# Splitting a matmul's first loads over two queues, and loading the last weight columns as float32

## Chip, cores and metric

The kernel runs on one core of a Trainium2 chip. The metric is the device time of one execution in microseconds (us), inputs and output in the chip's main memory. Before the change the median of three runs is 360.94 us (360.82 to 362.36).

## What is computed

x is 16 x 512 x 768 and w_qkv 768 x 2304, both float32. The product is cut into three column ranges, stacked as the output:

```python
qkv = np.matmul(x, w_qkv)
q, k, v = qkv[..., :768], qkv[..., 768:1536], qkv[..., 1536:]
return np.stack([q, k, v], axis=0).astype(np.float32)
```

## The kernel before

x is seen as 8192 rows of 768: 64 row tiles of 128, taken in 32 pairs p with r = 0 or 1. The contraction of 768 is cut into six slices j of 128. w's 2304 columns are five parts: four column blocks of 512 (q = 0 or 1 for a quad of two, c = 0 or 1 for the block within it) and a remainder of 256 columns in the middle, w_rem, held in two tiles of three slices each as bf16.

From pair 2 on, a pair and a quad are multiplied by a scheme of seven half-size products (`do`, lines 255 to 282, `product`, line 233) on sums of parts of x (`sums_x`) and of w (`sum_w`, line 112); products 1 and 2 use bf16, the others float32 data. The remainder columns are done plainly by `rem` and `rem_row` (lines 297 to 316): six bf16 matmuls of 256 columns for each row tile. Pairs 0 and 1 are multiplied plainly in bf16 by `block` (line 438), one column block at a time and slice by slice, as w's slices arrive.

The order of all instructions is written by hand: the program order of each engine is the order of the calls, and semaphores are put in where data depends. SyncE (SP) does little else than issue DMAs, so its program order is the order of its queue; ScalarE (ACT) and GpSimd (POOL) have queues of their own, and what they issue stands in line with their computing instructions. Hardware DMAs, whoever issues them, take eight completion semaphores in turn, so an issue also waits for the transfer eight before it.

What happens at the start, which the change and the prediction speak of:

- Line 397: DVE clears a tile of zeros, with which PE does matmuls for warming up (`busy`, line 423), eight at first and one or two between later steps.
- Lines 398 to 406: SP loads the four row tiles of pairs 0 and 1 (`load_row`, line 159). ScalarE issues two small loads, "touch", one of a few columns of w and one of a few columns of x's third row tile; nothing reads them.
- Lines 407 to 409: SP loads w's column block 0 in seven pieces, the first slice halved, and block 1 in six (`load_slices`).
- Line 410: SP loads the two row tiles of pair 2 in eight parts (`load_x_rows`, line 131), in another arrangement that DVE turns in blocks (`transpose`, line 148, instruction line 154).
- Lines 412 to 421: `hold` makes POOL wait for a transfer by copying one column of it (line 414). POOL waits for the first slice of w's block 1, then issues two loads of w_rem (line 419), which cast float32 to bf16 on the way. It waits for the first tile of pair 2 and goes on. SP loads quad 1's block 0 (`load_blocks`).
- Lines 495 to 514: for each of the four row tiles, DVE and ScalarE cast a half each to bf16 (`cast_row`, instruction lines 166 and 167), PE transposes six pieces (`turn_row`, line 184), and DVE and ScalarE copy the halves out of the PSUM banks (166, 167). DVE casts w's slices (line 434).
- Line 515: the first `block`, PE's line 456. Then four evacuations on ScalarE (line 446), two casts of w's slices by ScalarE (line 432), the second block (line 526), and `rem` for pairs 0 and 1 (line 529, PE's line 299).
- Lines 530 to 539: pair 2 is turned in two parts, ScalarE evacuates the second block's tiles, rounds each part of pair 2 to bf16 (`round_row`, line 200) and copies the remainder's results out (line 313).
- Lines 555 to 562: PE does the seven products of pair 2 and quad 0: 1 and 2 (evacuated at line 253), the remainder of pair 2, then product 6, which is added into the bank that line 253 has read (line 268).

From pair 3 on, `two` repeats one order for each pair, and `last` does the last.

Of the kernel before, what the change touches and what calls it, by code (L numbers as in the profile page):

```python
# [10 lines left out]
def kernel(  # L11
# [20 lines left out]
    nc = tc.nc  # L32
    P = 128
    G = 32
# [4 lines left out]
    KT = K // P  # L39
    KH = KT // 2  # L40
# [3 lines left out]
    REM = N3 - 4 * CB  # L44
    Q_OFF = (0, 2 * CB + REM)
    R_OFF = 2 * CB
    fp32 = mybir.dt.float32
    f32r = mybir.dt.float32r
    bf16 = mybir.dt.bfloat16
    ident = mybir.ActivationFunctionType.Identity  # L50
# [3 lines left out]
    x_flat = x.rearrange("b t h -> (b t) h")  # L54
# [7 lines left out]
    o_pool = ctx.enter_context(tc.tile_pool(name="o", bufs=5))  # L62
# [7 lines left out]
    m_pool = ctx.enter_context(tc.tile_pool(name="m", bufs=2))  # L70
# [6 lines left out]
    w_rem = [w_pool.tile([P, KH, REM], bf16, name="w_rem0"), None]  # L77
# [13 lines left out]
    def load_w(dst, j0, nj, off, cols):  # L91
        rows = w_qkv.rearrange("(p j) n -> p j n", j=KT)
        nc.sync.dma_start(dst, rows[:, j0:j0 + nj, off:off + cols])

    stage = {}

    def load_slices(c, cuts):
        t = tq_pool.tile([P, KT, CB], fp32, name="st0", tag="tq")
        stage[0, 0, c], stage[0, 1, c] = t[:, :KH, :], t[:, KH:, :]
        for j, nj, lo, hi in cuts:  # L100
            load_w(t[:, j:j + nj, lo:hi], j, nj, Q_OFF[0] + c * CB + lo, hi - lo)
# [10 lines left out]
    def sum_w(q, n):  # L112
        t1, t2, t3, t4 = ts[q]
        o, in0, in1 = {
            1: (t1, stage[q, 0, 1], stage[q, 0, 0]),
            2: (t2, stage[q, 1, 1], t1),
            3: (t3, stage[q, 1, 1], stage[q, 0, 1]),
            4: (t4, stage[q, 1, 0], t2),
        }[n]
        nc.vector.tensor_tensor(o, in0, in1, op=sub)  # L120

    xin, xf, xb, sr = {}, {}, {}, {}
# [8 lines left out]
    def load_x_rows(p, parts=range(8)):  # L131
        if p not in xin:
            xin[p] = xin_pool.tile([P, 2 * P // G, KC], fp32, name="xin")
        rows = x_flat[p * 2 * P:(p + 1) * 2 * P, :].rearrange("(g b) k -> b g k", b=G)
        for n in parts:
            r, i = divmod(n, 4)
            gs = slice(r * P // G, (r + 1) * P // G)
            nc.sync.dma_start(
                xin[p][i * G:(i + 1) * G, gs], rows[:, gs, i * KC:(i + 1) * KC]
            )  # L140
# [15 lines left out]

    def load_row(p, r):
        if r == 0:  # L160
            xin[p] = xin_pool.tile([P, 2, K], fp32, name="xin")
        row = (2 * p + r) * P
        nc.sync.dma_start(xin[p][:, r], x_flat[row:row + P, :])  # L163

    def copy_halves(dst, src):
        nc.vector.tensor_copy(out=dst[0], in_=src[0])
# [26 lines left out]
    act, dve = nc.scalar, nc.vector  # L193
# [202 lines left out]
    zero = xb_pool.tile([P, CB], bf16, name="zero", tag="xb")  # L396
    nc.vector.memset(zero[:], 0.0)
    load_row(0, 0)
    touch = m_pool.tile([P, 2, G], fp32, name="touch")
    nc.scalar.dma_start(touch[:, 0], w_qkv.rearrange("(p j) n -> p j n", j=KT)[:, 0, :G])  # L400
    nc.scalar.dma_start(touch[:, 1], x_flat[2 * P:3 * P, :G])
    nc.scalar.activation(tiny[:], zero[:, :1], ident)
    make_identity(nc, eye)
    load_row(0, 1)
    load_row(1, 0)
    load_row(1, 1)
    half = CB // 2
    load_slices(0, [(0, 1, 0, half), (0, 1, half, CB)] + [(j, 1, 0, CB) for j in range(1, KT)])
    load_slices(1, [(j, 1, 0, CB) for j in range(KT)])
    load_x_rows(2)  # L410

    def hold(src):
        mark = m_pool.tile([P, 1], fp32, name="mark")
        nc.gpsimd.tensor_copy(out=mark[:], in_=src)  # L414

    hold(stage[0, 0, 1][:, 0, :1])
    for h in range(2):
        rows = w_qkv.rearrange("(p j) n -> p j n", j=KT)[:, h * KH:(h + 1) * KH]
        nc.gpsimd.dma_start(w_rem[h][:], rows[:, :, R_OFF:R_OFF + REM])  # L419
    hold(xin[2][:, 0, :1])  # L420
    load_blocks(1, 0)

# [6 lines left out]
    def cast_j(q, c, w, j, eng=act, n=slice(0, CB)):  # L429
        src = stage[q, j // KH, c][:, j % KH, n]  # L430
        if eng is act:
            eng.activation(w[:, j, n], src, ident)
        else:
            eng.tensor_copy(out=w[:, j, n], in_=src)
# [86 lines left out]
    cast_j(0, 1, bt, 3, dve)  # L521
    cast_j(0, 1, bt, 4, act)
    cast_j(0, 1, bt, 5, act)
    sum_w(0, 2)
    nc.gpsimd.tensor_copy(out=b22[0][:], in_=stage[0, 1, 1])
    late = block(
# [119 lines left out]
```

## Time and profile before

| what | us |
|---|---|
| median of three runs | 360.94 (360.82 to 362.36) |
| the profiled execution | 360.69 |
| its span, first to last instruction | 358.9 |
| PE busy | 352.3 (98%) |
| DVE, ACT, POOL busy | 227.4, 185.7, 178.6 |
| first matmul of the first block (line 456) | 8.45 |
| first matmul of the remainder (line 299) | 18.85 |

The span is what the profile covers; 1.8 us of the execution lie around it. The page gives busy time of each engine, then the chain of work that ended last, then groups of instructions. The timeline lists instructions of one line together: start, duration, engine, line, operation, tiles written and read, shape, count, and in brackets the idle time of the engine before them and what ended it. A DMA is listed where it is issued; the list of issues, taken over a window that holds one, tells how long that one took to land. A view by stretches gives each engine's busy time, the granted clock, the share of the DMA engines in use and GB/s.

### The profile page before, as it was taken

How to read it: one execution, taken by the hardware profiler on the slowest of the kernel's cores; microseconds unless marked ns; L12 is line 12 of the kernel's file. 1: busy time of each engine (PE TensorE's matmuls, PEld its weight loads, DVE VectorE, ACT ScalarE, POOL GpSimd, SP SyncE). 2: the span in 40 equal slices, each digit the busy share in tenths (PEclk: the TensorE clock that was granted, in tenths of full speed). 3: DMA queues.
4: the chain of work that ended last, by engine and by line, in shares of the span. 5: the costliest groups of instructions: out<-in, count | busy, mean ns of one | idle time of the engine just before them, and what ended most of it. 6: DMA issues, size and time to landing. Idle time of an engine off the chain costs nothing.

```text
span 358.9 us, 5279 instructions
## 1 busy us (share of the span) xinstructions
PE 352.3 (98%) x1780; PEld 251.0 (70%) x1780; DVE 227.4 (63%) x244; ACT 185.7 (52%) x316; POOL 178.6 (50%) x187
## 2 busy tenths in 40 slices
PE   7999999999999999999999999999999999999995
PEld 3465577777777777777777777777777777777764
DVE  3879676676556675556676556676556676556643
ACT  5469644445444445444445544445545445545443
POOL 0221866435665444665444665444665444666420
PEclk9999999999999999999999999999999999999999
DMA  7999999798999999899999999988999899989767
GB/s 276 345 368 347 329 360 369 242 347 285 288 300 312 294 289 274 295 293 316 294 293 274 293 290 319 295 274 293 295 283 322 294 298 271 296 278 325 290 239 258
DMA packets 82106, 107.73 MB, mean 300 GB/s; under 512 B 5408, under 2 KB 62240, under 8 KB 82080
## 3 DMA queue, kind: packets, MB, share of 16 engines
q1 hardware_dynamic: 66672, 96.35, 82.4%
q10 hardware_dynamic: 14608, 10.65, 9.1%
q0 software_dynamic: 800, 0.39, 0.8%
q8 instruction: 14, 0.23, 0.3%
q14 instruction: 12, 0.10, 0.1%
HBM read 32.28 MB, written 75.50 MB: 300 GB/s over the span
## 4 chain that ended last, share of the span: by engine, by line
PE 92%; DMA 5%; ACT 1%; ACTq 0%; POOL 0%; SPq 0%; issue 0%
PE ps L244 78%; PE ps L299 11%; PE ps L456 3%; DMA w_rem<-in_w_qkv_dram 2%; DMA xin<-in_x_dram 1%; DMA st<-in_w_qkv_dram 1%; SPq L163 0%; ACT o L279 0%; ACTq L354 0%; POOL w_rem L419 0%; ACT orem L368 0%; POOL mark L414 0%; ACTq L370 0%; ACTq L368 0%
## 5 line engine op out<-in xcount | busy, mean ns | idle before, releaser
L244 PE MATMUL ps<-t,s 128*128 128x512 f32 x720 | 181.2, 399 | 0.0
L244 PEld LDWEIGHTS ps<-t,s 128*128 128x128 f32 x720 | 135.0, 188 | 30.7
L191 POOL CAST xb<-xf 128x1536 bf16<-128x1536 f32 x28 | 40.9, 1462 | 132.0 <-DVE xf L154 132.0
L276 DVE TENSOR_TENSOR o<-o,ps 128x512 f32<-128x512 f32 x58 | 39.9, 687 | 91.4 <-ACT o L275 91.4
L154 DVE STREAM_TRANSPOSE xf<-xin 128x1536 f32<-128x1536 f32 (+1 forms) x32 | 88.9, 2781 | 2.3 <-DMA xin<-in_x_dram 2.2
L244 PE MATMUL ps<-b,xb 128*128 128x512 bf16 x360 | 87.7, 380 | 0.0
L244 PEld LDWEIGHTS <-xb 128*128 128x128 bf16 x360 | 32.8, 98 | 37.3 <-issue 7.6
L269 ACT ACTIVATE o<-ps 128x512 f32<-128x512 f32 x60 | 35.9, 598 | 44.0 <-PE ps L244 41.3
L275 ACT ACTIVATE o<-ps 128x512 f32<-128x512 f32 x58 | 34.7, 598 | 44.3 <-PE ps L244 44.3
L282 DVE TENSOR_TENSOR o<-o,ps 128x512 f32<-128x512 f32 x60 | 41.2, 687 | 21.4 <-PE ps L244 20.2
L244 PE MATMUL ps<-b,s 128*128 128x512 f32 x180 | 50.4, 389 | 0.0
L279 ACT ACTIVATE o<-ps 128x512 f32<-128x512 f32 x60 | 35.9, 598 | 24.5 <-PE ps L244 21.6
L253 ACT ACTIVATE o<-ps 128x512 f32<-128x512 f32 x60 | 35.8, 597 | 24.4 <-DVE o L282 20.7
L299 PE MATMUL ps<-w_rem,xb 128*128 128x256 bf16 x384 | 47.5, 273 | 0.5 <-DMA w_rem<-in_w_qkv_dram 0.5
L299 PEld LDWEIGHTS <-xb 128*128 128x128 bf16 x384 | 37.2, 98 | 12.1 <-issue 1.4
L266 DVE TENSOR_TENSOR o<-o,ps 128x512 f32<-128x512 f32 x60 | 37.8, 672 | 2.0 <-ACT o L253 1.3
L244 PEld LDWEIGHTS ps<-b,s 128*128 128x128 f32 x180 | 33.8, 188 | 7.1
L212 POOL TENSOR_TENSOR s<-s,xf 128x384 fp32r<-128x384 f32 x29 | 29.4, 1013 | 2.3
L215 POOL TENSOR_TENSOR s<-xf,s 128x384 fp32r<-128x384 f32 x29 | 29.5, 1016 | 0.0
L213 POOL TENSOR_TENSOR s<-xf 128x384 fp32r<-128x384 f32 x29 | 29.4, 1013 | 0.0
L313 ACT ACTIVATE orem<-ps 128x512 f32<-128x512 f32 x31 | 18.5, 596 | 21.0 <-PE ps L299 21.0
L211 POOL TENSOR_TENSOR s<-xf 128x384 fp32r<-128x384 f32 x29 | 29.3, 1011 | 0.0
(45 smaller groups left out, 119.1 us busy)
## 6 DMA issues: line engine op xcount, KB each, us to landing
out_dram<-o SPq DMA_DIRECT2D x62, 768.0 KB, 4.9
out_dram<-o SPq DMA_DIRECT2D x65, 256.0 KB, 4.0
xin<-in_x_dram SPq DMA_DIRECT2D x62, 192.0 KB, 6.9
xin<-in_x_dram ACTq DMA_DIRECT2D x50, 192.0 KB, 4.2
out_dram<-orem SPq DMA_DIRECT2D x31, 256.0 KB, 5.8
st<-in_w_qkv_dram SPq DMA_DIRECT2D x11, 256.0 KB, 5.0
st<-in_w_qkv_dram SPq DMA_DIRECT2D x3, 768.0 KB, 10.1
xin<-in_x_dram SPq DMA_DIRECT2D x4, 384.0 KB, 4.3
```

Of the source, the lines that this page charges most:

```text
L154: nc.vector.transpose(turned[:, g:g + n], rows[:, g:g + n])
L191: nc.gpsimd.tensor_copy(out=xb[p][:], in_=xf[p][:])
L215: 4: lambda g: g.tensor_tensor(s[:, 4], a12, s[:, 2], op=sub),
L244: nc.tensor.matmul(ps[:], lhs[j], rhs[j], start=(start and j == 0), stop=(j == KH - 1), skip_group_check=True,)
L253: nc.scalar.activation(u.o[:, 0, :CB], u.x[:], ident)
L266: nc.vector.tensor_tensor(c11, c11, u.z[:], op=add)
L269: nc.scalar.activation(c12, u.x[:], ident)
L275: nc.scalar.activation(c22, u.x[:], ident)
L276: nc.vector.tensor_tensor(c22, c22, u.y[:], op=add)
L279: nc.scalar.activation(c21, u.x[:], ident)
L282: nc.vector.tensor_tensor(c12, c12, u.y[:], op=add)
L299: nc.tensor.matmul(ps, xb[p][:, j, r * P:(r + 1) * P], w_rem[j // KH][:, j % KH, :], start=(j == 0), stop=(j == KT - 1), skip_group_check= ...
```

## The change

- Of the four row tiles of pairs 0 and 1, the second and fourth (p, 1) are loaded by ScalarE's queue, ahead of its touch; the first and third by SP, with no other load between them and w's slices.
- The touch of x's third row tile is left out; the touch of w stays.
- w's remainder columns are loaded by SP as float32, in two loads of three slices, into a tile of the output pool. They stand behind w's block 1 and ahead of pair 2's rows.
- ScalarE casts them to bf16 into w_rem, with two instructions that stand behind its casts of w's slices 4 and 5 and ahead of the evacuations of the second block.
- POOL's wait for the first slice of block 1 and its two casting loads are gone; its wait for pair 2's first tile stays.

```diff
-    def load_row(p, r):
+    def load_row(p, r, eng=nc.sync):
...
-        nc.sync.dma_start(xin[p][:, r], x_flat[row:row + P, :])
+        eng.dma_start(xin[p][:, r], x_flat[row:row + P, :])
...
     load_row(0, 0)
-    touch = m_pool.tile([P, 2, G], fp32, name="touch")
+    load_row(0, 1, nc.scalar)
+    load_row(1, 0)
+    load_row(1, 1, nc.scalar)
+    touch = m_pool.tile([P, 1, G], fp32, name="touch")
     nc.scalar.dma_start(touch[:, 0], w_qkv.rearrange("(p j) n -> p j n", j=KT)[:, 0, :G])
-    nc.scalar.dma_start(touch[:, 1], x_flat[2 * P:3 * P, :G])
     nc.scalar.activation(tiny[:], zero[:, :1], ident)
     make_identity(nc, eye)
-    load_row(0, 1)
-    load_row(1, 0)
-    load_row(1, 1)
...
     load_slices(1, [(j, 1, 0, CB) for j in range(KT)])
+    st_rem = o_pool.tile([P, KT, REM], fp32, name="str", tag="o")
+    for h in range(2):
+        load_w(st_rem[:, h * KH:(h + 1) * KH], h * KH, KH, R_OFF, REM)
     load_x_rows(2)
...
-    hold(stage[0, 0, 1][:, 0, :1])
-    for h in range(2):
-        rows = w_qkv.rearrange("(p j) n -> p j n", j=KT)[:, h * KH:(h + 1) * KH]
-        nc.gpsimd.dma_start(w_rem[h][:], rows[:, :, R_OFF:R_OFF + REM])
     hold(xin[2][:, 0, :1])
...
     cast_j(0, 1, bt, 4, act)
     cast_j(0, 1, bt, 5, act)
+    act.activation(w_rem[0][:], st_rem[:, :KH], ident)
+    act.activation(w_rem[1][:], st_rem[:, KH:], ident)
     sum_w(0, 2)
```

## The prediction

> **What bounds the kernel now.** I read the page first: PE is busy for 352.3 of 358.9 us and the chain that ended last is 92% PE. Then the waits of PE between 19.9 us and 350 us, to see whether anything holds PE up once it runs. The answer has one row, and the timeline shows that wait ending at 19.82, at the very start of the stretch:
>
> ```profile
> PE ps L299 <- DMA w_rem<-in_w_qkv_dram: 0.5, 1, 0.5
> ```
>
> So from 19.82 us on the time is PE's own work, which the change leaves as it is. Whatever it does must happen in the first 20 us, or be a new wait behind them. The chain of waits up to there:
>
> ```profile
> 2.12 5.36 DMA xin<-in_x_dram
> ...
> 7.50 4.54 DMA st<-in_w_qkv_dram
> 12.03 0.05 issue
> 12.09 0.44 POOL mark L414
> 12.53 0.86 POOL w_rem L419
> 13.38 6.39 DMA w_rem<-in_w_qkv_dram
> 19.78 0.04 issue
> 19.82 2.45 PE ps L299 x21
> ```
>
> The columns are start, duration and what. The second half of w_rem is issued by POOL at 13.38 and lands at 19.77; PE's remainder products (L299) wait for it. The timeline of PE around that point, and of the first block:
>
> ```profile
> 8.08 0.54 PE L184 MATMUL ps<-eye,xc 128*128 128x128 bf16 x6 [0.34 <-ACT xc L167]
> 8.45 5.38 PE L456 MATMUL ps<-b,xb 128*128 128x256 bf16 x27
> 13.67 5.34 PE L456 MATMUL ps<-both,xb 128*128 128x512 bf16 x24
> 18.85 0.49 PE L299 MATMUL ps<-w_rem,xb 128*128 128x256 bf16 x3
> 19.82 2.45 PE L299 MATMUL ps<-w_rem,xb 128*128 128x256 bf16 x21 [0.48 <-DMA w_rem<-in_w_qkv_dram]
> ```
>
> PE has no gap from 8.45 to 19.1: 24 matmuls fill 13.67 to 18.85, 0.216 each. The remainder's 21 matmuls fill 19.82 to 22.11, 0.109 each, so its first three were done streaming at 18.85 + 3 x 0.109 = 19.18, and **the stall on w_rem is 19.82 - 19.18 = 0.64 us**. The end can move by two things only: this stall, and the start of the first block, now 8.45, which moves all behind it one for one while nothing else is late.
>
> **Part 1: the stall.** The last slice of w's second column block is issued at 10.11 and takes 5.5 us to land, 15.6, the last stretch of it among other packets; the slices before landed 0.6 to 0.7 apart, so without that it is 15.2. Behind it now come two loads of 384 KB in pieces of 1 KB. The nearest rows: a 128 KB half slice with the same pieces landed 0.39 after the one before it (7.82, 8.21), so 3 x 0.39 = 1.17 each; the 256 KB slices give 1.5 x 0.62 = 0.93; x's rows of 384 KB landed 1.2 apart. I take 1.15, as the 1 KB row is nearest: the halves land at 16.35 and **17.5** (17.1 to 17.6), against 18.4 and 19.77.
>
> ScalarE's two new casts are 128x768 float32 to bf16, the shape of L200's row (0.84 and 0.85 us). ScalarE ends its last w cast at 16.31, so they run 16.4 to 17.25 and 17.5 to 18.35. PE wants the second half three matmuls into the remainder, at 19.18 or later: 0.8 us to spare. The 0.64 goes. POOL's mark (0.44) and two issues (0.86, 0.78) go too; POOL was waiting (10.8 us before the mark), so they are worth nothing by themselves.
>
> What stands behind the casts on ScalarE: the evacuations of the second block, at 17.11 before and now 18.35 to 19.6, then x's third pair rounded by L200. ScalarE idled 0.79 before the former and 0.86 before the latter, so 1.65 of the 1.7 us of casts is covered, unless the data for L200 is late.
>
> It is later: x's third pair of row tiles queues behind w's remainder on SP. Its first four loads (96 KB, pieces of 768 B) ended at 17.46 and the next four at 20.7, sharing the DMA engines with POOL's casting transfer:
>
> ```profile
> 15.50:19.00 3.50, 3.50 (x19) 1.61 (x17) 3.41 (x3) 2.01 (x4) 1.39 (x2) 1.00 1.31 239
> ...
> 20.50:27.00 6.50, 6.50 (x46) 4.67 (x44) 6.01 (x8) 5.08 (x10) 0.87 (x1) 1.00 1.04 404
> ```
>
> The last number is GB/s, in two stretches with the DMA engines full: 239 beside the casting transfer, 404 without. Alone these small loads land 0.27 apart (eight of pair 3 between 30.92 and 32.78). So the first four now land at 17.5 + 4 x 0.27 = **18.55** (18.2 with fast remainder loads; 19.5 at the 0.47 spacing of the stretch above), 1.1 later than before, and all eight at 19.65, 1.0 earlier. What follows, by rows: the turn (L154) starts at once, L200 1.64 after that (17.58 to 19.22), so at 20.21; the first remainder copy (L313) 0.75 later, 20.96, against 21.00 before, when it waited for PE. From there ScalarE is busy back to back to the end of L253, at 24.28 before and 24.24 now. PE's product 6 (line 268, recorded on L244), at 24.63 before, adds into the bank that L253 reads, and PE follows ScalarE by 0.05 (4.63 to 4.68): 24.29 at the earliest, which **caps the gain at 0.34 us** (0.7 if the rows land at 18.2, minus 0.6 if at 19.5). DVE's second turn ends 0.6 earlier than before, so DVE's sums cap nothing. Later w blocks (768 KB, landing 1.9 apart) land about 1.7 earlier (the first at 19.65 + 1.9 = 21.6 against 23.4); PE did not wait for them.
>
> **Part 2: the start of the first block.** The four row tiles of x are 384 KB each. They landed at 4.1, 5.1, 6.3 and 7.5 us, issued 0.47 apart; from 2.5 to 7.5 us the DMA share is 0.99 at 359 GB/s. They are bound by the engines, not by SP's 0.39 to 0.43 per issue, so two queues cannot bring the last row much forward. What changes is the order: tiles 0 and 2 on SP run beside 1 and 3 on ScalarE's queue. The touch packets shared in turn with row 0's, so I assume that the queues take turns. If they start together, tiles 0 and 1 land at about 5.0, 2 and 3 at about 7.4; but the touch of 16 KB, issued with row 0, landed 0.2 after its 384 KB, so ScalarE's queue seems to start later. I take 4.5, 5.0, 6.8 and 7.25 (a little off for the touches now behind the rows). The touch of x was waited for by nothing. The touch of w now comes behind two rows, too late to be of use to w's first slices; if those lose 0.25 us for it, as x's first row did (2.0 to 2.5 us, DMA share 0.49), they land at 8.1 instead of 7.8 and are cast by 8.6, just hidden.
>
> From each landing to the first block, by ScalarE's own spacing in the timeline:
> - last row: 0.03 + cast 0.52 + 0.05 + six transposes 0.37 = 0.97 (7.48 to 8.45 checks): 8.2.
> - third row: cast, 0.44 to the copy of row 1, 0.39 to the last cast, then 0.52 + 0.05 + 0.37: 1.80, so 6.8 + 1.8 = **8.6**.
> - first row: 0.03 + 1.15 + 0.39 + 1.14 + 0.39 + 0.94 = 4.04, so 8.55.
>
> So the block starts at 8.6, **0.15 later** (bounds: 8.2 if SP's rows keep their pace, 0.25 earlier; 9.2 with the third row at 7.4, 0.75 later). w's slices are queued earlier, and each is needed 0.86 after the one before (four matmuls) but lands every 0.65; that hides SP's waits for the transfer eight before. PE's side of the gain is 0.64 - 0.15 = 0.49.
>
> The Trainium skill, "DMA: Bandwidth & Descriptors", section "Issuing engines are not separate DMA queues", says that transfers started from several engines share the same 16 engines and that spreading them saves issue time only. By it part 2 cannot gain more than the issue spacing, and the sum would stand; the 0.99 share agrees.
>
> **Sum.** The smaller of 0.49 and 0.34: PE's steady work starts 0.34 us earlier. The profiled execution took 360.69 (358.9 span and 1.8 around it), so 360.35; it lies 0.25 under the median of 360.94 (360.82 to 362.36), so against the median **360.6**. A measurement of this kernel can tell about 0.5%, 1.8 us, from no change.
>
> **Rivals.**
> 1. The order of the rows eats the stall (0.2): block start at 9.05 to 9.2, 0.6 to 0.75 later. For it: ScalarE's chain is in order, and two rows that land together make it do two casts and a copy in a row. Net 0: **360.9**.
> 2. Slower, by x's third pair (0.17): the rows of 768 B behind the remainder land later than 18.9, from where the ScalarE chain above is later than PE was. At 19.5 it is 0.6 behind: **361.5**. Against it: the casting transfer that slowed them is gone.
> 3. PE's clock (0.05): matmuls up to 4.06 us start 0.43 apart, later ones 0.216. The first row lands 0.4 later, so PE idles about 0.65 us instead of 0.24 before the first transposes, and more between the later ones. If the clock fell back for as long as the first slow stretch (1.19 to 3.96), 2.8 us would do 1.4 us of work: 360.6 + 1.4 = **362.0**. The Trainium skill, "TensorE: Matmul & The Clock Gate", Part 1 on the HAM clock gate, says the clock halves after an idle window of about 3.4 us; no idle time here comes near it.
> 4. Everything on the good side (0.08): the rows land at 18.2, the block starts at 8.2 and the cap loosens to 0.7: **360.2**.
>
> Forecast 0.5. The range 359.9 to 361.7 takes in the bounds of both parts and leaves out rival 3 and the tails. Faster by over 0.5% would be below 359.1, more than the whole stall and the earliest block start (0.89) give: 0.02. Slower by over 0.5% is over 362.7, beyond even rival 3 as priced: 0.04. Within: 0.94.
>
> **What would show it.** PE's L299 without a wait on w_rem; POOL's L414 for w gone; first L456 at 8.6 (wrong if under 8.2 or over 9.2); x's third pair turned from about 18.6; the new casts 0.85 each; PE waiting, if at all, ahead of product 6 for ScalarE near 24.3; PE's steady stretch 0.34 earlier at the same length. A wait of PE after 26 us, or a clock row below 1.00 in the first block, would prove the working wrong.

## The result, and the profile after

The change makes the kernel slower: 362.53 us (median of 22 runs, 361.56 to 363.16) against 361.36 (median of 22 runs of the kernel before beside them, 360.33 to 363.15). The ratio is 1.0032, 95% interval 1.0024 to 1.0040, so **1.17 us more**. The forecast was 0.34 us less, and the range ended at 361.7. The change moved the time by 0.3%, so it stays within half a percent either way, but it lies outside the range and on the other side.

The profiled execution took 362.19 us with a span of 360.4, 1.5 more than before. The granted clock is 0.999. The chain of waits at the start, which answers to the one shown of before:

```profile
1.18 5.74 DMA xin<-in_x_dram
6.92 0.02 issue
6.93 0.33 SPq L93
7.26 0.04 issue
7.31 4.60 DMA st<-in_w_qkv_dram
11.90 0.02 issue
11.92 6.67 DMA str<-in_w_qkv_dram
18.59 0.02 issue
18.61 3.85 DMA xin<-in_x_dram
...
22.58 1.58 DVE xf L154
24.16 0.02 issue
24.18 0.84 ACT xb L200
25.02 0.49 ACT orem L313
25.51 0.49 ACT o L253
26.01 0.04 issue
26.05 1.65 PE ps L244 x6
```

Before, this chain ended at the remainder (19.82). Now it runs through two loads that wait for earlier ones (6.93 is SP's issue of w's slice 4, released by a row tile; 18.61 is the last part of pair 2's rows, released by the second half of the remainder), then through DVE's turn, ScalarE's rounding, the remainder's copy and line 253 to PE's product 6. PE and its neighbours around that place, from the timeline (PEld is PE's loading of weights, on a row of its own):

```profile
8.73 5.35 PE L454 MATMUL ps<-b,xb 128*128 128x256 bf16 x26
...
13.92 5.34 PE L454 MATMUL ps<-both,xb 128*128 128x512 bf16 x24
...
16.84 0.84 ACT L522 ACTIVATE w_rem<-str 128x768 bf16<-128x768 f32 x1 [0.28 <-DMA str<-in_w_qkv_dram]
18.61 0.84 ACT L523 ACTIVATE w_rem<-str 128x768 bf16<-128x768 f32 x1 [0.93 <-DMA str<-in_w_qkv_dram]
...
19.10 2.87 PE L299 MATMUL ps<-w_rem,xb 128*128 128x256 bf16 x24
...
19.94 1.61 DVE L154 STREAM_TRANSPOSE xf<-xin 128x768 f32<-128x768 f32 x1 [1.98 <-DMA xin<-in_x_dram]
...
22.48 1.47 PE L244 MATMUL ps<-b,xb 128*128 128x512 bf16 x5 [0.52 <-ACT xb L200]
22.58 1.57 DVE L154 STREAM_TRANSPOSE xf<-xin 128x768 f32<-128x768 f32 x1 [1.03 <-DMA xin<-in_x_dram]
...
25.08 0.83 PE L299 MATMUL ps<-w_rem,xb 128*128 128x256 bf16 x6 [0.47 <-ACT xb L200]
...
26.05 1.23 PEld L244 LDWEIGHTS ps<-t,s 128*128 128x128 f32 x6 [0.42 <-ACT o L253]
```

From the timeline of before, the two turns of pair 2's rows and product 6:

```profile
17.58 1.60 DVE L154 STREAM_TRANSPOSE xf<-xin 128x768 f32<-128x768 f32 x1
...
20.85 1.57 DVE L154 STREAM_TRANSPOSE xf<-xin 128x768 f32<-128x768 f32 x1 [1.67 <-DMA xin<-in_x_dram]
...
24.63 1.64 PE L244 MATMUL ps<-t,s 128*128 128x512 f32 x6
```

The stall on w_rem is gone (19.10, no bracket). In its place PE waits for the rounded first half of pair 2 (22.48), for the second half (25.08) and for line 253 (26.05). Product 6 starts at 26.05 against 24.63, 1.42 later; that is the 1.5 us of the span but for 0.1, and PE has no other wait of note behind it. From the start of product 6 to the end of the span it is 334.2 to 334.5 us in all 16 kernels of this document, so what a kernel loses or gains can be read from that start.

The rows land late: the two halves of pair 2 at 19.82 and 22.46, against 17.46 and 20.66 before. The DMA also differs earlier, in the stretch 9.5 to 12 us of the view by stretches (the last two numbers are the DMA share and GB/s). First before, then after the change:

```profile
9.50:12.00 2.50, 2.50 (x13) 1.13 (x12) 1.68 (x4) 0.00 (x0) 0.00 (x0) 1.00 1.04 394
...
9.50:12.00 2.50, 2.45 (x13) 1.10 (x12) 1.12 (x4) 0.00 (x0) 0.00 (x0) 1.00 0.97 320
```

The engines are as busy (0.97 against 1.04) and move a fifth less: single reads of w take longer. In the trace's packets, reads of 2 KB take 84 ns in the usual case; from 8 to 12.5 us, 12 of them took over 250 ns (the longest 1500), against 5 before.

### The profile page after: what moved, and what is told of

It reads as the page before. It is cut to its first block, busy times and chain, and to the rows that moved or that the text cites. A ratio compares the mean times of both kernels' runs of the same rounds, so it can differ in the third digit from the quotient of the medians.

```text
span 360.4 us, 5247 instructions
## 1 busy us (share of the span) xinstructions
PE 351.4 (98%) x1749; PEld 250.9 (70%) x1780; DVE 228.7 (63%) x244; ACT 186.7 (52%) x318; POOL 176.4 (49%) x184
## 4 chain that ended last, share of the span: by engine, by line
PE 90%; DMA 6%; ACT 1%; issue 1%; ACTq 1%; DVE 0%; SPq 0%; DVEq 0%
PE ps L244 77%; PE ps L299 10%; PE ps L454 3%; DMA xin<-in_x_dram 3%; DMA str<-in_w_qkv_dram 2%; DMA st<-in_w_qkv_dram 1%; DVE xf L154 0%; ACT o L279 0%; ACTq L354 0%; ACT xb L200 0%; ACT orem L368 0%; ACT o L253 0%; ACT orem L313 0%; ACTq L163 0%; ACTq L370 0%
## 5 line engine op out<-in xcount | busy, mean ns | idle before, releaser
L244 PE MATMUL ps<-b,xb 128*128 128x512 bf16 x331 | 85.3, 380 | 2.1 <-ACT xb L200 0.5
L211 POOL TENSOR_TENSOR s<-xf 128x384 fp32r<-128x384 f32 x29 | 30.8, 1062 | 0.0
L313 ACT ACTIVATE orem<-ps 128x512 f32<-128x512 f32 x31 | 18.5, 596 | 21.3 <-PE ps L299 20.4
L213 POOL TENSOR_TENSOR s<-xf 128x384 fp32r<-128x384 f32 x29 | 29.4, 1014 | 0.0
```

What stands on the lines that cost most here:

```text
L211: 1: lambda g: g.tensor_tensor(s[:, 1], a21, a22, op=add),
L244: nc.tensor.matmul(ps[:], lhs[j], rhs[j], start=(start and j == 0), stop=(j == KH - 1), skip_group_check=True,)
```

## The experiments

Each kernel ran beside the kernel before, whose median was 361.3 to 361.4 in every set; "loss" is the difference of the medians. The counts, landings and waits of a kernel are each read from one profile of it.

**The two parts, each alone, and ScalarE's part in it.** e1 is the kernel before with the row split alone; e2 with the remainder's part alone; e3 is the change without the remainder's loads, e4 the change with the casts on GpSimd.

```diff
 e1: the diff of the rows and touches; w_rem by GpSimd as before
 e2: the diff of w_rem; rows and touches as before
 e3 (on the change)
-    for h in range(2):
-        load_w(st_rem[:, h * KH:(h + 1) * KH], h * KH, KH, R_OFF, REM)
+    nc.gpsimd.memset(st_rem[:], 0.0)
 e4 (on the change)
-    act.activation(w_rem[0][:], st_rem[:, :KH], ident)
-    act.activation(w_rem[1][:], st_rem[:, KH:], ident)
...
+    for h in range(2):
+        nc.gpsimd.tensor_copy(out=w_rem[h][:], in_=st_rem[:, h * KH:(h + 1) * KH])
     hold(xin[2][:, 0, :1])
```

> The kernel before with only the row split: tiles 2 and 4 of x on ScalarE's queue and the touch of x gone; the remainder of w stays with GpSimd's casting loads. Queue theory (pair 2's rows land late because they stand behind the remainder's loads, and PE then waits for ScalarE's rounding of pair 2): only the later first block counts, 0.28 us in the profile of the change, so +0.2 to +0.5 us against before, first block near 8.7, no wait of PE on L200. Start theory (the split and the missing touch delay all of w's slices, and that is the loss): most of the loss is here, +0.9 to +1.3 us.

> The kernel before with only the remainder's part: two float32 loads on SyncE's queue ahead of pair 2's rows, cast by ScalarE; rows and touches as before. Queue theory: first block at 8.45, no wait on w_rem, but pair 2's rows land after 19 us and PE waits about 1.2 to 1.5 us in total for L200 and L253; +0.6 to +1.0 us against before. Start theory: the stall of 0.64 goes and little is lost, -0.6 to 0 us.

> The change without the two loads of the remainder: their staging tile is filled with zeros by GpSimd, so the remainder's columns of the output are zeros; ScalarE's two casts stay where they are. Queue theory: pair 2's first half lands near 17, nothing waits for it, and what is left is the stall gone and the block 0.28 later: -0.2 to -0.5 us against before. ScalarE theory (the casts themselves push evacuations and rounding back): the loss stays, +0.9 to +1.3 us. Start theory: it stays too.

> The change with the remainder's two casts moved from ScalarE to GpSimd, ahead of its wait for pair 2. Queue theory: pair 2's rows land as late as in the change, near 19.8 and 22.5, so the loss stays, +0.9 to +1.4 us against before. ScalarE theory: ScalarE is free of 1.7 us ahead of the evacuations, so the loss goes, -0.4 to +0.3 us.

| run | us | loss | ratio, 95% interval |
|---|---|---|---|
| e1, row split alone | 362.17 | +0.77 | 1.0021 (1.0011 to 1.0031) |
| e2, remainder alone | 361.92 | +0.52 | 1.0012 (1.0000 to 1.0024) |
| e3, change without the remainder's loads | 360.92 | -0.48 | 0.9988 (0.9974 to 1.0002) |
| e4, change with the casts on GpSimd | 362.18 | +0.78 | 1.0018 (1.0008 to 1.0029) |

The two parts add up (1.0021 and 1.0012 to the 1.0032 of both), so there are two causes, though not by the same waits: e1 still has the stall on w_rem, which the change has not. e1 lost more than the queue theory gave it and less than the start theory; e2 and e4 lost about 0.1 less than the queue theory's least. The first block does not tell why e1 lost: it begins at 9.03 here, but at 8.80 in e2, whose rows are loaded as before. The loss is later. PE's waits in e1, behind the first transposes:

```profile
PE ps L299 <- DMA w_rem<-in_w_qkv_dram: 0.8, 1, 0.8
PE ps L455 <- ACT both L431: 0.2, 1, 0.2
```

Line 431 is the cast of w's slices 4 and 5 of the second column block. ScalarE does it late since the slice lands late:

```profile
16.94 0.63 ACT L431 ACTIVATE both<-st 128x512 bf16<-128x512 f32 x1 [0.56 <-DMA st<-in_w_qkv_dram]
```

The second block takes 5.72 us for it in e1 (14.22 to 19.94) instead of 5.18, and the stall on w_rem, worked out as in the prediction, is 0.94 instead of 0.64: 0.84 more in the two. The stretch 9.5 to 12 us is 300 GB/s in e1 and 391 in e2.

In e2 PE waits for the rounding of pair 2 as in the change, though its rows are loaded as before, and product 6 starts at 25.57:

```profile
24.60 0.83 PE L299 MATMUL ps<-w_rem,xb 128*128 128x256 bf16 x6 [0.50 <-ACT xb L200]
25.57 1.66 PE L244 MATMUL ps<-t,s 128*128 128x512 f32 x6
```

e3 shows that the loads of the remainder, and not the casts, are the other cause: without them the time falls by some 1.6 us, though the casts are still there and PE now waits 0.9 for the late slice. e4 lost less than the change, by 0.4, but the intervals overlap; a small share of the casts is not excluded. In its profile PE still waits 0.41 for the rounding of pair 2.

**Why w's slices come late after the row split.** Three suspects: SP's issue of slice 4, which waits for a row tile (until 6.93 in the change; it is issued at 5.65 before); the touch of x that is gone; the touch of w that comes later. By the semaphores in the trace the tile is the fourth (landed at 6.92), and not the third (6.49), as I took it to be in the expectations. g1 leaves out the touch of x alone, g2 merges slices so that no issue of the first block waits for the third or the fourth tile, g3 puts the touch of w first. g4 is on the other part: it loads the remainder as float32 by GpSimd's queue.

```diff
 g1 (on before)
-    nc.scalar.dma_start(touch[:, 1], x_flat[2 * P:3 * P, :G])
 g2 (on e1)
-    load_slices(0, [(0, 1, 0, half), (0, 1, half, CB)] + [(j, 1, 0, CB) for j in range(1, KT)])
+    load_slices(0, [(0, 1, 0, half), (0, 1, half, CB), (1, 1, 0, CB), (2, 2, 0, CB), (4, 2, 0, CB)])
 g3 (on e1): the touch of w ahead of load_row(0, 0) and of ScalarE's rows
 g4 (on before, with the change's two casts by ScalarE)
-        nc.gpsimd.dma_start(w_rem[h][:], rows[:, :, R_OFF:R_OFF + REM])
+        nc.gpsimd.dma_start(st_rem[:, h * KH:(h + 1) * KH], rows[:, :, R_OFF:R_OFF + REM])
```

> The kernel before with only the touch of x's third row tile left out. Wait theory (what delays w's slices after the row split is that SyncE's issue of slice 4 waits for the third row tile, which shares its completion semaphore, until 6.5 to 6.9 us): here every such wait is for an earlier transfer than before, so no loss, within 0.2 us of before, slice 4 issued before 6.3. Touch theory (the early touch of x makes the reads that follow quicker): +0.2 to +0.5 us.

> The kernel before with the row split, and slices 2 and 3, and 4 and 5, of w's first column block loaded together, two transfers fewer, so that none of that block's issues waits for the third row tile. Wait theory: slices 4 and 5 are issued near 5.3, the stretch 9.5 to 12 us is back near 390 GB/s (300 to 330 with the split alone), PE waits for no cast in the second block; +0.1 to +0.4 us against before instead of +0.77. Touch theory: the stretch stays near 320 GB/s and the loss stays, +0.6 to +0.9 us.

> The kernel before with the row split, but the touch of w first in ScalarE's queue, ahead of its two rows. It also moves each wait for an earlier transfer by one: slice 4 now waits for the second row tile. Touch theory: the stretch 9.5 to 12 us is back near 390 GB/s, and here alone of the two split kernels; +0.2 to +0.5 us against before. Wait theory: the stretch is back in both, slice 5 is still issued after 6.5; +0.2 to +0.6 us.

> The kernel before with the remainder loaded by GpSimd's queue at the same place as before, but as float32, and cast by ScalarE as in the change. Queue theory (the loss of the remainder's part is that pair 2's rows stand behind it on SyncE's queue): pair 2's first half lands near 17.5 as before, no wait of PE on L200; the remainder lands near 18.9 and is cast by 19.8, so PE waits for it about as long as before: -0.3 to +0.2 us. If casting in the transfer was what slowed the other transfers, the stretch 15.5 to 19 us moves clearly more than 239 GB/s of written bytes.

| run | us | loss | ratio, 95% interval | GB/s, 9.5 to 12 us |
|---|---|---|---|---|
| g1, no touch of x | 361.49 | +0.21 | 1.0004 (0.9996 to 1.0013) | 404 |
| g2, split, slices merged | 362.21 | +0.93 | 1.0021 (1.0013 to 1.0030) | 363 |
| g3, split, touch of w first | 361.57 | +0.29 | 1.0008 (0.9996 to 1.0020) | 368 |
| g4, remainder float32 by GpSimd | 364.54 | +3.26 | 1.0082 (1.0060 to 1.0104) | 400 |

The touch of x does not bring the slow reads: g1 has none over 250 ns between 8 and 12.5 us, and 404 GB/s. Its time lies at the edge of the two expectations, and the interval takes in no loss at all. The wait is not the cause either: in g2 slices 4 and 5 are issued at 5.33 and the loss stays. There the merged slices 2 and 3 land at 11.11, three us after slice 1, so that PE waits:

```profile
PE ps L455 <- DVE b L433: 0.9, 1, 0.9
```

Merging also makes slice 2 wait for slice 3, so g2 alone leaves a doubt; but in m1 below slice 4 is issued at 6.00, and the slow reads and a loss are there too. g3 fell between the theories: less is lost, but the reads still stall (8 over 250 ns between 8 and 12.5 us), and PE waits 0.5 for a late slice. My expectation for g4 missed by 3 us: the remainder landed at 20.4 and 22.4, later than with the cast in the transfer, and PE waited 2.7 us for ScalarE's casts of it. Pair 2's first half landed at 19.2 and not near 17.5, so g4 does not test the queue theory. The stretch 15.5 to 19 us moved 239 GB/s of written bytes, the same as before, and SyncE's loads 0.33 MB of it against 0.44 before, so they were no quicker without the casting.

**What the remainder's loads cost, and what else might help.** k1 puts only the second row tile on ScalarE's queue. k2 is e2 without the two loads, k3 is e2 with the second half of pair 2 rounded by GpSimd, and k4 is the kernel before with GpSimd's loads one slice earlier.

```diff
 k1 (on e1)
-    load_row(1, 1, nc.scalar)
+    load_row(1, 1)
 k2 (on e2): as e3
 k3 (on e2)
-    round_row(2, 1, act)
+    round_row(2, 1, nc.gpsimd)
 k4 (on before)
-    hold(stage[0, 0, 1][:, 0, :1])
+    hold(stage[0, 1, 0][:, KH - 1, :1])
```

> The kernel before with only the second row tile on ScalarE's queue (ahead of the touch of w; no touch of x), the other three on SyncE's. Straggler theory (rows going out on two queues at once leave single DMA engines with stalled reads of w's slices some 2 to 4 us later, which PE then waits for): with half of the overlap, some of it is left: 4 or more reads of 2 KB over 250 ns between 9.4 and 12.5 us, +0.2 to +0.8 us against before. If the fourth tile, beside w's first slices, is what does it: no more than 3 such reads and within 0.2 us of before.

> The remainder's part alone (rows and touches as before), without its two loads: GpSimd fills the staging tile with zeros, so the remainder's columns of the output are zeros; ScalarE's casts stay. Queue theory: pair 2's first half lands near 16.8, its second near 18.2, PE has no wait behind the first block; -0.5 to -0.9 us against before, and 1.0 to 1.4 us less than with the loads (+0.5). ScalarE theory: the casts still push ScalarE back, 0 to +0.5 us.

> The remainder's part alone, with the second half of pair 2 rounded by GpSimd instead of ScalarE, so that ScalarE's evacuation at line 253 no longer stands behind that half. Queue theory: PE still waits for the second half's rounding ahead of the second half of its remainder products, but not for line 253 any more: about 0.3 us better than the +0.5, so 0 to +0.4 us against before. If PE's wait for line 253 costs nothing of its own: +0.4 to +0.6 us.

> The kernel before, with GpSimd's casting loads of the remainder held for the last slice of w's first column block instead of the first slice of the second, one slice of 0.6 us earlier. If the stall of PE on w_rem (0.64 us in the profile of before) can be had back by starting these loads earlier: they land near 19.2, the stall is 0 to 0.2 and the time -0.3 to -0.6 us against before. If the casting transfer then slows w's last slices and pair 2's rows: PE waits there instead, within 0.2 us or slower.

| run | us | loss | ratio, 95% interval |
|---|---|---|---|
| k1, second tile alone on ScalarE's queue | 361.22 | -0.14 | 0.9991 (0.9977 to 1.0005) |
| k2, remainder's part without its loads | 360.48 | -0.88 | 0.9969 (0.9957 to 0.9982) |
| k3, remainder's part, GpSimd rounds | 361.99 | +0.63 | 1.0007 (0.9994 to 1.0021) |
| k4, GpSimd's loads earlier | 361.29 | -0.07 | 0.9999 (0.9986 to 1.0013) |

k2 puts a price on the second cause: 0.52 + 0.88 = **1.4 us for two loads ahead of pair 2's rows**, against a gain of 0.88 that the remainder would bring if its loads were free (k2 has no such bytes to move at all, so this is the most). The same loads put behind pair 2's rows were not tried. Pair 2's rows land by 17.8 and 19.1 in k2, by 19.4 and 22.0 in e2, and PE has no wait in k2 behind its transposes. k3 is inconclusive in time, and slower than both its expectations; in its profile the wait for line 253 is gone and DVE's sum takes its place, so several engines stand one behind the other there:

```profile
PE ps L244 <- ACT xb L200: 0.5, 1, 0.5
PE ps L244 <- DVE s L212: 0.4, 1, 0.4
PE ps L299 <- POOL xb L202: 0.3, 1, 0.3
```

k4 shows that the stall of before is not had back by an earlier start: the second half of the remainder lands as late against the block as ever, and PE waits 0.45 in its profile. None of these kernels is clearly faster than the one before and whole.

**What brings the stalled reads about.** m1 puts only the fourth tile on ScalarE's queue. m2 is e1 with the touch of w replaced by a load into eight partitions, meant to set the DMA engines apart (skew is one of the staging tiles of w).

```diff
 m1 (on e1)
-    load_row(0, 1, nc.scalar)
+    load_row(0, 1)
 m2 (on e1)
-    nc.scalar.dma_start(touch[:, 0], w_qkv.rearrange("(p j) n -> p j n", j=KT)[:, 0, :G])
+    nc.scalar.dma_start(skew[:8].rearrange("p j n -> p (j n)"),
+                        x_flat[:16, :].rearrange("(p r) k -> p (r k)", r=2))
```

> The kernel before with only the fourth row tile on ScalarE's queue (the touch of w behind it, no touch of x). With one tile on the second queue, the second one, w's slices came in time and nothing was lost. If it takes the fourth tile, which runs beside w's first slices: 4 or more reads of 2 KB over 250 ns between 8 and 12.5 us, +0.3 to +0.9 us against before. If it takes two tiles on the second queue: no more than 3 such reads, within 0.2 us of before.

> The row split alone, with the touch of w replaced by a load of 48 KB into eight partitions behind ScalarE's two rows, so that some DMA engines start w's slices later than others. Step theory (with the split all 16 engines finish each transfer within 0.4 to 0.6 us of each other, against 0.8 without, and reads that run in step collide): the 16 completions of w's slices 1 to 3 spread over 0.7 us or more, no more than 3 reads of 2 KB over 250 ns between 8 and 12.5 us, 0 to +0.3 us against before. If the step has nothing to do with it: 6 or more such reads and +0.6 to +0.9 us as with the split.

m1 took 361.90 us (+0.60; 1.0019, 1.0008 to 1.0029), m2 362.57 (+1.27; 1.0033, 1.0021 to 1.0046). Reads of 2 KB over 250 ns between 8 and 12.5 us, counted in one profile of each kernel:

| kernels | such reads |
|---|---|
| rows all on SP: before, g1, e2, g4, k2, k3, k4 | 5, 0, 3, 1, 4, 1, 1 |
| second tile on ScalarE's queue: k1 | 4 |
| fourth tile on ScalarE's queue: m1 | 16 |
| both: the change, e1, e3, e4, g2, g3, m2 | 12, 18, 13, 18, 19, 8, 19 |

So the row split brings the stalls in this stretch, and the fourth tile on the second queue is enough for it. It is not the only thing that brings such reads: between 17 and 24 us there are 32, 20 and 24 of them in e2, k2 and k3, whose rows all came by SP, and 1 before.

How far the stalls make up the lost time is less certain. PE waits 0.2 to 0.9 us for a late slice in the profiles of e1, e3, g2, g3 and m2, but for none in those of m1, e4 and the change; in g4, with all rows on SP, it waits 0.2 for one. m1's profile is that of its fastest run (361.21); its first block begins at 9.47, since the third tile lands at 7.70, and k4's begins at 9.52 with all rows on SP. Where m1 loses its 0.60 is not shown.

m2 did not test the step theory: its load did not set the engines apart (the first 13 of 16 completions of slice 1 came within 0.20 us, against 0.58 before), and it kept the stalls. e1 speaks against that theory: it has 18 such reads, and the same 13 completions are spread over 0.56 us, nearly as before. **What makes the reads stall stays open.**

## Why the prediction was wrong, step by step

Two steps failed. The row split was priced by the start of the first block alone (0.15 us), and it cost 0.77 by itself. And the first half of pair 2's rows was put at 18.55 and landed at 19.82, which made the cap by ScalarE a loss.

- **What bounds the kernel: right.** From product 6 on it takes 334.35 us in the profile of the change, 334.27 before. PE's clock, rival 3, played no part: the granted clock is 0.999 and the second block takes 5.18 us as before. That its 362.0 is the forecast nearest to the time is chance.
- **The stall on w_rem: right.** It went, and k2 puts the gain without the loads at 0.88 (the stall alone was 0.64). The casts took 0.84 each, as L200's row gave.
- **The start of the first block: right in size.** 8.73, forecast 8.6, but by another row than the one it was read from. The tiles landed at 4.69, 4.86, 6.49 and 6.92, where I took 4.5, 5.0, 6.8 and 7.25; the first row decided (4.69 + 4.04 = 8.73), and not the third (6.49 + 1.80 = 8.29). And the base was one profile: in the eight profiles with the rows as before or only the second tile moved, the block begins between 8.45 and 9.52, and the 8.45 I started from is the earliest of them. The base median also moved, from 360.94 with three runs to 361.36 with 22; that is 0.42 us of the 1.93 between 360.6 and 362.53.
- **"w's slices are queued earlier ... that hides SP's waits": this failed.** The issue of slice 4 did wait, until 6.93, and slice 4 landed 1.64 after slice 3 instead of 0.65 (9.63, 11.27); g2 shows that the wait is not the cause. What I put at nothing is what the split does to the loads behind the rows: reads of w stall, and e1, with its slices late, lost 0.77. I priced only the order in which the rows land. Why the reads stall is open. The Trainium skill, "DMA: Bandwidth & Descriptors", section "Issuing engines are not separate DMA queues", says that spreading saves issue time only; I let it stand as no gain, where the runs show a loss.
- **The landing of pair 2's rows: the mechanism was right, the size was not.** Forecast 18.55 and 19.65, in the profile 19.82 and 22.46. The terms: w's last slice at 15.76 instead of 15.2; the remainder's halves 1.06 and 1.77 apart instead of 1.15 each; the first four parts 1.23 instead of 1.08. In e2, without the row split, they are 15.63, then 1.03 and 1.44, then 1.31, which gives 19.41: so 0.86 of the 1.27 belongs to the remainder's part and 0.41 came with the split. The 0.4 that I took off for other packets beside the last slice was not there to be had. The last two parts, which I costed at the spacing of the others, were issued only at 16.84 and 18.61, when the two halves of the remainder had landed: an issue waits for the transfer eight before it, and I had called that hidden for w's slices and not worked it out for these.

  The last of them was also late by one of its 16 completions (told in the last section); along ScalarE's chain both together cost no more than the 0.30 that it waits for the second half (24.18). The 239 GB/s that I set against 404 count the casting transfer's bytes as written; as read, they make 351, so there was less to win back there than I thought.
- **The cap by ScalarE: right in place.** Product 6 starts 0.05 after line 253 ends, as worked out; the rounding of the first half came 1.38 later (21.59 instead of 20.21), and ScalarE, which I took to be busy back to back from there, waited 0.30 for the second half: 26.05 instead of 24.29. Rival 2 was this case, with 18.9 as the decisive point and 0.6 us as its price at 19.5. Rows at 17.8 brought no such wait (k2), and with rows at 19.4 e2 lost 0.52. It got 0.17, and the row split's loss came on top; rival 1 has the split only as a first block that begins at 9.05 or later, and it began at 8.73.

## What to carry to other kernels

Where the DMA engines are full, loads put ahead of others delay these, and the price is read from whoever needs what stands behind, all the way to PE: 768 KB put the halves of pair 2's rows back by 1.6 and 2.9 us (e2 against k2), and the price, 1.4 us, was more than the stall that went. An issue that reuses a completion semaphore waits for an earlier transfer, so a large transfer holds back the issue of the eighth after it (16.84 and 18.61 in the change). That the bytes stay the same does not make it safe to move loads to a second queue: time it by itself.

## What the runs showed of the hardware

- Reads of 2 KB that usually take 84 ns took 250 to 1500 ns in stretches of some us. From 8 to 12.5 us there were 8 to 19 of them where the fourth row tile had come by a second queue, and at most 5 elsewhere; the stretch 9.5 to 12 us had the engines 0.90 to 1.05 busy at 300 to 368 GB/s there, and 1.04 to 1.06 at 386 to 404 elsewhere. Later, with one queue, e2 had 32 between 17 and 24 us.
- A load of instructions goes through the same DMA engines and seems to hold one of them up: 16 KB took 1185 ns from 19.55 us in the change's profile. The seventh part of pair 2's rows had 13 of its 16 completions by 20.64 and the last at 22.11; in e2 the load came at 19.06, and that part had 13 by 20.05 and the last at 21.58. Before, it came at 19.88 and the eighth part ended at 20.46 and 20.66; the transfer behind it had 13 by 22.22 and the last at 23.33. In e4, with a load at 19.56, no completion stands out in this way. This is read from four profiles and is no experiment. The page counts these loads in its list of queues:

```profile
q8 instruction: 14, 0.23, 0.3%
```

- Beside SyncE's small loads, GpSimd's loads landed later when they carried float32 (384 KB written for each half in g4, 192 KB as bf16 before): 7.1 and 8.2 us after their issue, against 5.9 and 6.4, in one profile of each.
